# Moving the weight buffers of an fp32r decoder block by 448 bytes: stationary operands 64 bytes behind the moving ones, modulo 512

## The chip, the cores and the metric

The kernel runs on one core of a Trainium2 chip. The metric is the device time of one execution in microseconds (us). Three runs of the kernel before gave 2026.83, 2027.70 and 2027.73 us, a median of 2027.7 us. One more execution was profiled; it has a time of its own, 2027.62 us, and its first to last instruction span 2025.9 us.

## The reference

One layer of a hybrid decoder block over 2048 tokens of 1024 channels, all in float32:

```python
h = rmsnorm(x, norm_g[l])
proj = jnp.einsum("bsd,de->bse", h, w_in[l])          # 1024 -> 7680
glu_in, conv_gate, q, k, v, attn_gate, merge_logits = jnp.split(proj, SPLIT_POINTS, axis=-1)
c = conformer_conv(glu_in, ...)                       # GLU, 31 taps depthwise, layernorm, SiLU
y_conv = jnp.einsum("bsc,cd->bsd", c * jax.nn.silu(conv_gate), w_conv_out[l])
a = sliding_window_attention(q, k, v, attn_sinks[l])  # rope before it; window 128, 16 heads, 4 kv heads
y_attn = jnp.einsum("bsa,ad->bsd", a * jax.nn.silu(attn_gate), w_attn_out[l])
merged = g_conv * y_conv + g_attn * y_attn            # sigmoid gates
x = x + jnp.einsum("bsd,de->bse", merged, w_out[l])
return rmsnorm(x, final_norm_g)
```

## The kernel before, in words

**Tiling.** The tokens are done in two sweeps of 1024 (`T`), each as two halves of 512 (`TH`). The contraction of 1024 channels is cut into 8 chunks of 128 (`KC`). Every product keeps float32 accuracy by splitting both operands into a high part, rounded to fp32r, and a low part, the rest: high times high, high times low and low times high are added up in one PSUM bank. So a projection of 128 output channels over one half is 8 x 3 = 24 matmuls, with a weight load ahead of each; over both halves it is 48 (`project`, lines 267 to 293, the matmul at L281).

**What is stationary, what moves.** In `project` the stationary operand (the weight load) is 128 x 128 numbers of `whi` or `wlo`, and the moving operand is 128 x 512 numbers of `hT` (the normalized input, transposed), `aT` (the gated attention output) or `uT` (the gated convolution output). Per sweep `project` runs for 60 tiles of `w_in`, 8 of `w_attn_out` (named `ya`) and 8 of `w_conv_out` (`yc`): 76 tiles, 152 in the two sweeps. The last product, with `w_out` (L885, named `o`), has it the other way: stationary is `mT`, moving is `wo`, and both lie in slots. So do both operands of the attention products `sc` (L572) and `ov` (L622).

**Memory.** Four pools lie behind each other in each partition: `const`, `slots`, `stage`, `work`. `const` holds `ident_r` (from byte 2,176), `ones` (from 2,688), the parameters and `v_halo` (from 5,952). `slots` is a set of named slots of 4,096 bytes (three of 4,608) which `slot` hands out again and again (lines 81 to 91): `hT`, `aT`, `uT`, `mT`, `wo`, `qk`, `pt`, `vt` and the rest lie there. `stage` has four buffers each of `raw` (a weight tile as it comes from memory), `whi` and `wlo`, 2,048 bytes each. `work` has the half rows `t2k` (five of 2,048 bytes) and small things. In bytes modulo 512 the pools begin like this:

| what | first byte | modulo 512 |
|---|---|---|
| `ident_r`, `ones` (const) | 2,176 and 2,688 | 128 |
| `v_halo` (const) | 5,952 | 320 |
| first slot | 9,024 | 320 |
| last slot, tag `c5` | 182,592 | 320 |
| stage: `raw`, `whi`, `wlo` | 186,688 | 320 |
| work: first `t2k` | 215,424 | 384 |

All slots, all rows of 512 float32 and all columns of 128 float32 are multiples of 512 bytes, so within a pool every operand keeps the number of its pool. The distance that the change is about is that of the stationary operand behind the moving one, modulo 512. In `project` it is 0.

**Order.** TensorE's instructions stand in the order in which the program writes them; a clock of planned time (`Line`, with 0.2275 us per matmul) sets in between them the transposes and the attention's products as they come due, and ScalarE, VectorE and GpSimd get their work at the same points. A weight tile's load from memory, its rounding on ScalarE (L253) and its low part on GpSimd (L242 through `split_lo`) are issued one item ahead of the matmuls that use it (`prefetch` in `project`).

The layernorm's sums over channels are matmuls too (L666): `ones` is stationary and half rows of `work` (`csumh`, `csuml`, `vsumh`, `vsuml`) move.

Of the kernel before, what the change touches and what calls it, by code (L numbers as in the profile page):

```python
# [19 lines left out]
P = 128  # L20
# [33 lines left out]
def hybrid_block(ctx: ExitStack, tc: tile.TileContext, x, par_d, w_in, w_conv, sinks, w_attn, w_out,  # L54
# [22 lines left out]
    C = [f"c{i}" for i in range(8)]  # L77
    X = [f"x{i}" for i in range(3)]
    WIDE = {"c6", "c7", "a14"}

    def slot(tag, shape, dt, name):
        n = int(np.prod(shape[1:]))
        full = 1024 + P if tag in WIDE else 1024
        t = slots.tile([P, full], dt, tag=tag, name=name)
        v = t[:, 0:n]
        if len(shape) == 3:
            v = v.rearrange("p (a b) -> p a b", b=shape[2])
        elif len(shape) == 4:
            v = v.rearrange("p (a b c) -> p a b c", b=shape[2], c=shape[3])
        return v  # L90
# [11 lines left out]
    def load_first(half):  # L102
        xs = []
        for j in range(4):
            r0 = (4 * half + j) * P
            xs.append(slot(A[7 * half + j], [P, D], F32, f"xf{half}_{j}"))
            nc.sync.dma_start(out=xs[-1], in_=x2[r0:r0 + P, :])
        return xs
# [4 lines left out]
    ident_r = const.tile([P, P], F32R, name="ident_r")  # L113
    ident = f(ident_r)
    ident_0 = slot(A[4], [P, P], F32, "ident_0")
    make_identity(nc, ident_0)
    dve.tensor_copy(out=ident_r, in_=ident_0)
    ones_0 = slot(A[5], [P, P], F32, "ones_0")
    dve.memset(ones_0, 1.0 / D)
    ones = const.tile([P, P], F32R, name="ones")  # L120
# [844 lines left out]
```

## Time and profile before

| | |
|---|---|
| median of three runs | 2027.7 us |
| the profiled execution | 2027.62 us, span 2025.9 us |
| TensorE matmul busy (PE) | 2004.9 us, 99% |
| weight loads (PEld) | 1666.9 us, 82% |
| VectorE (DVE) | 1324.1 us, 65% |
| ScalarE (ACT) | 1026.0 us, 51% |
| GpSimd (POOL) | 403.4 us, 20% |
| granted TensorE clock | 0.999 |
| memory traffic | 175 GB/s over the span |

Each row of the group view reads: line, engine, operation, what is written from what (moving operand, then stationary one, for a matmul), shape, count, then busy time in us, the mean ns of one, and the engine's idle time just before them. A matmul's row has a modelled end, so its duration covers the way through the array and overlaps with the next one; the pace of a stream of matmuls is the distance of their starts, and that is read from the timeline, whose first column is the start in us, rounded to 0.01, and whose last is how many instructions of one kind a row holds.

### The profile page before, as it was taken

How to read it: one execution, taken by the hardware profiler on the slowest of the kernel's cores; microseconds unless marked ns; L12 is line 12 of the kernel's file. 1: busy time of each engine (PE TensorE's matmuls, PEld its weight loads, DVE VectorE, ACT ScalarE, POOL GpSimd, SP SyncE). 2: the span in 40 equal slices, each digit the busy share in tenths (PEclk: the TensorE clock that was granted, in tenths of full speed). 3: DMA queues.
4: the chain of work that ended last, by engine and by line, in shares of the span. 5: the costliest groups of instructions: out<-in, count | busy, mean ns of one | idle time of the engine just before them, and what ended most of it. 6: DMA issues, size and time to landing. Idle time of an engine off the chain costs nothing.

```text
span 2025.9 us, 27562 instructions
## 1 busy us (share of the span) xinstructions
PE 2004.9 (99%) x9256; PEld 1666.9 (82%) x9256; DVE 1324.1 (65%) x1965; ACT 1026.0 (51%) x2313; POOL 403.4 (20%) x336
## 2 busy tenths in 40 slices
PE   7999999999999999999999999999999999999998
PEld 6888888888888888888888888888888888888887
DVE  4968779988994365123668678699888924431324
ACT  6312577767777463123533225777777764621222
POOL 2335332333323223241001120110111100001200
PEclk9999999999999999999999999999999999999999
DMA  7445655555566757445343556555555577564432
GB/s 252 146 146 167 212 172 159 161 170 180 161 189 213 245 188 249 150 151 178 134 147 132 167 181 196 159 178 177 176 157 174 175 231 260 176 229 140 152 114 83
DMA packets 265821, 355.91 MB, mean 176 GB/s; under 512 B 28112, under 2 KB 126544, under 8 KB 265680
## 3 DMA queue, kind: packets, MB, share of 16 engines
q1 hardware_dynamic: 265680, 354.16, 53.9%
q8 instruction: 73, 1.20, 0.2%
q14 instruction: 68, 0.56, 0.1%
HBM read 234.51 MB, written 119.54 MB: 175 GB/s over the span
## 4 chain that ended last, share of the span: by engine, by line
PE 94%; DVE 4%; DMA 1%; issue 0%; ACT 0%; SPq 0%; POOL 0%; DVEq 0%; ACTq 0%; POOLq 0%
PE mm_ma L281 9%; PE o L885 9%; PE mm_mc L281 9%; PE mm_yc L281 9%; PE mm_ya L281 9%; PE mm_ga L281 9%; PE mm_gb L281 8%; PE mm_cg L281 8%; PE mm_ag L281 6%; PE mm_q_a L281 4%; PE mm_q_b L281 4%; PE sc L572 3%; DVE acc L396 3%; PE ov L622 2%; PE mm_v L281 2%; PE tpp L602 1%
## 5 line engine op out<-in xcount | busy, mean ns | idle before, releaser
L396 DVE SCALAR_TENSOR_TENSOR acc<-glu,par,acc 128x1024 f32<-128x1024 f32 x464 | 595.9, 1284 | 6.2
L885 PE MATMUL o<-wo,mT 128*128 128x512 f32 x768 | 178.3, 391 | 0.0
L885 PEld LDWEIGHTS o<-wo,mT 128*128 128x128 f32 x768 | 143.1, 188 | 29.2
L281 PE MATMUL mm_cg<-hT,whi_cg 128*128 128x512 f32 x512 | 159.6, 393 | 0.0
L281 PE MATMUL mm_ma<-hT,whi_ma 128*128 128x512 f32 x512 | 159.6, 393 | 0.0
L281 PE MATMUL mm_ga<-hT,whi_ga 128*128 128x512 f32 x512 | 159.4, 392 | 0.2 <-ACT whi_ga L253 0.2
L281 PE MATMUL mm_ag<-hT,whi_ag 128*128 128x512 f32 x512 | 159.4, 392 | 0.0
L281 PE MATMUL mm_gb<-hT,whi_gb 128*128 128x512 f32 x512 | 159.2, 392 | 0.0
L281 PE MATMUL mm_mc<-hT,whi_mc 128*128 128x512 f32 x512 | 157.9, 389 | 0.0
L281 PE MATMUL mm_yc<-uT,whi_yc 128*128 128x512 f32 x512 | 157.7, 389 | 0.0
L281 PE MATMUL mm_ya<-aT,whi_ya 128*128 128x512 f32 x512 | 157.7, 389 | 0.0
L613 POOL TENSOR_SCALAR_AFFINE_SELECT pc<-pt 128x1024 fp32r<-128x1024 f32 x60 | 65.7, 1094 | 422.1 <-DVE pt L242 413.4
L281 PEld LDWEIGHTS mm_ya<-aT,whi_ya 128*128 128x128 f32 x512 | 96.1, 188 | 20.1
L281 PEld LDWEIGHTS mm_yc<-uT,whi_yc 128*128 128x128 f32 x512 | 96.1, 188 | 20.0
L281 PEld LDWEIGHTS mm_mc<-hT,whi_mc 128*128 128x128 f32 x512 | 95.9, 188 | 20.0
L281 PEld LDWEIGHTS mm_ga<-hT,whi_ga 128*128 128x128 f32 x512 | 94.4, 188 | 19.1 <-ACT whi_ga L253 0.6
L281 PEld LDWEIGHTS mm_gb<-hT,whi_gb 128*128 128x128 f32 x512 | 94.6, 188 | 18.6
L281 PEld LDWEIGHTS mm_ag<-hT,whi_ag 128*128 128x128 f32 x512 | 94.2, 188 | 18.3
L281 PEld LDWEIGHTS mm_ma<-hT,whi_ma 128*128 128x128 f32 x512 | 94.1, 188 | 18.1
L281 PEld LDWEIGHTS mm_cg<-hT,whi_cg 128*128 128x128 f32 x512 | 94.0, 188 | 18.1
L592 ACT ACTIVATE ss<-ss,st 128x128 f32<-128x128 f32 x256 | 99.7, 390 | 11.2 <-DVE st L587 10.6
L281 PE MATMUL mm_ga<-hT,wlo_ga 128*128 128x512 f32 x256 | 99.9, 390 | 0.7 <-POOL wlo_ga L242 0.7
(364 smaller groups left out, 4244.5 us busy)
## 6 DMA issues: line engine op xcount, KB each, us to landing
qk<-d_q SPq DMA_DIRECT2D x256, 64.0 KB, 2.2
d_a<-ss SPq DMA_DIRECT2D x128, 128.0 KB, 1.9
aT<-d_a SPq DMA_DIRECT2D x32, 512.0 KB, 5.7
qk<-d_k SPq DMA_DIRECT2D x240, 64.0 KB, 2.0
raw_gb<-in_w_in_dram SPq DMA_DIRECT2D x34, 256.0 KB, 3.4
raw_ga<-in_w_in_dram SPq DMA_DIRECT2D x34, 256.0 KB, 3.3
raw_ag<-in_w_in_dram SPq DMA_DIRECT2D x32, 256.0 KB, 3.6
d_ag<-ag SPq DMA_DIRECT2D x32, 256.0 KB, 2.2
```

Of the source, the lines that this page charges most:

```text
L281: pe.matmul(out=ps, lhsT=a, rhs=b, start=(k == 0 and i == 0), stop=(k == KC - 1 and i == 2))
L396: dve.scalar_tensor_tensor(out=to, in0=glu[c][:, j:j + T], scalar=tap(c, j), in1=acc[c], op0=ALU.mult, op1=ALU.add)
L572: pe.matmul(out=o, lhsT=q[:, h, :], rhs=r, start=(j == 0), stop=(j == 1))
L592: act.activation(out=sb[:, h, :], in_=sb[:, h, :], func=AF.Exp, scale=SCALE, bias=ngm[:, h:h + 1], accum_out=den[:, h:h + 1])
L602: pe.transpose(out=tpp[:, h, :], in_=sb[:, h, :], identity=ident)
L613: pool.affine_select(out=pc, in_=f(pt), pattern=[[0, 2], [0, GQ], [1, P]], compare_op=ALU.is_ge, fill=0.0, base=0, channel_multiplier=-1)
L622: pe.matmul(out=ov, lhsT=vv, rhs=pp[:, i % 2], start=(i == 0), stop=(i == nm - 1))
L885: pe.matmul(out=ps, lhsT=a[:, c0:c0 + P], rhs=r, start=(k == 0 and i == 0), stop=(k == KC - 1 and i == 2))
```

## The change

The slot with the tag `c5` is the last of the pool in memory. It gets 112 float32, that is 448 bytes, more; what is put into it stays as it is.

```diff
     def slot(tag, shape, dt, name):
         n = int(np.prod(shape[1:]))
-        full = 1024 + P if tag in WIDE else 1024
+        full = 1024 + (P if tag in WIDE else 112 if tag == C[5] else 0)
         t = slots.tile([P, full], dt, tag=tag, name=name)
```

All that lies behind that slot moves up by 448 bytes: `stage` begins at 187,136 (256 modulo 512) and the first `t2k` of `work` at 215,872 (320 modulo 512). `const` and all slots stay where they are. No instruction is added, removed or reordered.

## The prediction

> **What bounds the kernel now.** I read the page first: the busy shares, the clock and the chain that ended last.
>
> ```profile
> span 2025.9 us, 27562 instructions
> PE 2004.9 (99%) x9256; PEld 1666.9 (82%) x9256; DVE 1324.1 (65%) x1965; ACT 1026.0 (51%) x2313; POOL 403.4 (20%) x336
> PEclk9999999999999999999999999999999999999999
> PE 94%; DVE 4%; DMA 1%; issue 0%; ACT 0%; SPq 0%; POOL 0%; DVEq 0%; ACTq 0%; POOLq 0%
> ```
>
> TensorE works without a break at its full granted clock, and 94% of the chain that sets the end is its own queue. So the time is the number of matmuls times the pace at which one follows the other, and a change of place in memory matters if it changes that pace. The timeline of TensorE gives the pace in the attention output product, where nothing else is mixed in:
>
> ```profile
> 800.02 0.62 PE L281 MATMUL mm_ya<-aT,whi_ya 128*128 128x512 f32 x2
> 800.47 0.39 PE L281 MATMUL mm_ya<-aT,wlo_ya 128*128 128x512 f32 x1
> ...
> 809.31 0.39 PE L281 MATMUL mm_ya<-aT,wlo_ya 128*128 128x512 f32 x1
> 809.54 0.62 PE L281 MATMUL mm_ya<-aT,whi_ya 128*128 128x512 f32 x2
> ```
>
> Between 800.02 and 809.54 lie 42 matmuls (14 groups of three), 9.52 us, so 226.7 ns each. How much of that is the streaming of 512 columns? Two shapes tell it, in the group view:
>
> ```profile
> L281 PE MATMUL mm_ya<-aT,whi_ya 128*128 128x512 f32 x512 | 157.7, 389 | 0.0
> L572 PE MATMUL sc<-qk 128*128 128x256 f32 x480 | 67.8, 283 | 1.4 <-DVE pt L242 1.3
> L281 PEld LDWEIGHTS mm_ya<-aT,whi_ya 128*128 128x128 f32 x512 | 96.1, 188 | 20.1
> L281 PE MATMUL mm_cg<-hT,whi_cg 128*128 128x512 f32 x512 | 159.6, 393 | 0.0
> ```
>
> 256 columns more take 389 - 283 = 106 ns more, 0.414 ns a column, so 512 columns stream in 212 ns and 226.7 - 212 = 14.7 ns of each step are something else. The attention scores, with half the columns, show the same surcharge:
>
> ```profile
> 500.48 1.11 PE L572 MATMUL sc<-qk 128*128 128x256 f32 x8
> 501.43 0.40 PE L281 MATMUL mm_cg<-hT,whi_cg 128*128 128x512 f32 x1
> ```
>
> Eight of them pass in 0.95 us, 119 ns each, 13 ns over their 106. A weight load takes 188 ns, hidden beside a step of 226.7. So about 15 ns per matmul do not depend on its length; both operands have the same distance (0) in all these groups. Whether those 15 ns are two reads of the memory getting in each other's way, or a fixed price of changing the weights, is what the change asks.
>
> **The change part by part.** It adds no instruction. It changes one distance: of the 76 tiles per sweep of `project`, 48 matmuls each, two sweeps, that is 7,296 matmuls, from 0 to 64 bytes behind. One nanosecond of pace is worth 7.3 us. The 768 matmuls of the output product, the attention products and all tiles in slots keep their distance. I sum up term by term.
>
> *Pace of the 7,296 matmuls.* Nowhere does the trace show a long run at a distance other than 0, but it shows four short ones: the layernorm sums. There `ones` (128 modulo 512) is stationary and a half row of `work` (384) moves, and the last of each four runs while `whi_mc` (320) is loaded for the next, which is 64 bytes behind 384, the very distance of the change.
>
> ```profile
> 697.31 0.39 PE L281 MATMUL mm_mc<-hT,wlo_mc 128*128 128x512 f32 x1
> 697.54 0.39 PE L666 MATMUL lnmu<-csumh,ones 128*128 128x512 f32 x1
> 697.77 0.39 PE L666 MATMUL lnmu<-csuml,ones 128*128 128x512 f32 x1
> 698.00 0.40 PE L666 MATMUL lnmu<-csumh,ones 128*128 128x512 f32 x1
> 698.23 0.39 PE L666 MATMUL lnmu<-csuml,ones 128*128 128x512 f32 x1
> 698.46 0.61 PE L281 MATMUL mm_mc<-hT,whi_mc 128*128 128x512 f32 x2
> 698.91 0.39 PE L281 MATMUL mm_mc<-hT,wlo_mc 128*128 128x512 f32 x1
> ```
>
> The step from 697.31 to 697.54 has `hT` moving and `ones` being loaded, 192 bytes behind: 0.23 us, the usual step as far as 10 ns tell. The four steps from 697.54 to 698.46 take 0.92 us, 230 ns each, 3.3 ns above the usual 226.7; then two steps take 0.45, the usual pace. Nothing here is faster than at distance 0. Read as a price of distance, 3.3 ns x 7,296 = 24 us. But the same slow stretch appears at distance 0, after transposes:
>
> ```profile
> 648.89 0.40 PE L281 MATMUL mm_ma<-hT,wlo_ma 128*128 128x512 f32 x1
> 649.12 0.62 PE L281 MATMUL mm_ma<-hT,whi_ma 128*128 128x512 f32 x2
> 649.58 0.39 PE L281 MATMUL mm_ma<-hT,wlo_ma 128*128 128x512 f32 x1
> 649.81 0.61 PE L281 MATMUL mm_ma<-hT,whi_ma 128*128 128x512 f32 x2
> 650.27 0.39 PE L281 MATMUL mm_ma<-hT,wlo_ma 128*128 128x512 f32 x1
> 650.49 0.61 PE L281 MATMUL mm_ma<-hT,whi_ma 128*128 128x512 f32 x2
> ```
>
> From 648.89 to 649.81 four steps take 0.92 us, just as in the layernorm; from 649.81 to 650.49 three take 0.68, the usual 227. So a disturbance of the stream is paid for by a few slow steps, then the stream falls back into its pace, and the layernorm's four are what such a recovery looks like whatever the distance is. (These spells are why `mm_cg`, mixed with attention, has a mean of 393 ns and `mm_ya` 389.) I take 0 ns for the pace, the value that the nearest steady rows support, with bounds of -14.7 ns (the whole surcharge goes) and +3.3 ns (the stretch at 230 never ends). [...]
>
> *Weights ready in time.* `raw`, `whi`, `wlo` and the half rows shift too, so ScalarE, GpSimd and the DMAs touch other addresses.
>
> ```profile
> L253 ACT CAST whi_yc<-raw_yc 128x512 fp32r<-128x512 f32 x32 | 19.8, 620 | 61.1 <-PE mm_ya L281 34.3 <-issue 22.6 <-DMA wlo_yc<-d_lo 4.2
> L296 ACT CAST uT<-lcg 128x512 fp32r<-128x512 f32 x32 | 19.3, 620 | 28.1 <-DVE lcg L719 27.8
> PE mm_ga L281 <- POOL wlo_ga L242: 0.7, 1, 0.7
> PE mm_ga L281 <- ACT whi_ga L253: 0.2, 1, 0.2
> ```
>
> A cast from 320 to 320 takes 620 ns and one from 384 to 320 takes 620 too, so for ScalarE the place costs nothing, and I take the same for the others. The waits view of TensorE shows 0.9 us in all for weights that were late, in the first tiles of the kernel. Term: 0; if loads became 10 ns slower each, they would still be an item ahead, and cost nothing.
>
> *Transposes and layernorm.* Their stationary or moving tiles in `stage` and `work` shift. The 16 layernorm matmuls cost 3.3 ns each above the pace: 0.05 us, the most that can be won there.
>
> *Sum.* Against the profiled execution: 2027.62 us + 0, its span of 2025.9 with 1.7 us around it. The median of the runs, 2027.7, is the same to 0.1 us. Forecast: 2027.6 us, its own range 2024 to 2032.
>
> **The rivals.** *Collision at equal distance, faster.* The surcharge is a collision of two reads that start at the same number modulo 512, and the weights 64 bytes behind avoid it in part or altogether. For: 14.7 and 13 ns at 512 and 256 columns, at distance 0 in each case; a fixed price that fits one short overlap at the start of each matmul. Against: the step at distance 192 and those at 256 were no faster. If half goes, 7.3 ns x 7,296 = 54 us, 1974 us; if all goes, 14.7 x 7,296 = 107 us, 1920 us. The next engine leaves room for the first: over both attention stages
>
> ```profile
> 240.00:680.00 440.00, 438.59 (x2104) 366.81 (x2103) 360.08 (x552) 315.10 (x771) 135.26 (x113) 1.00 0.57 179
> 1240.00:1700.00 460.00, 460.00 (x2201) 385.05 (x2200) 356.89 (x568) 327.41 (x794) 49.83 (x41) 1.00 0.59 184
> ```
>
> VectorE (the third busy time) is busy 360 of 440 and 357 of 460 us, 82% and 78%; 3% fewer us raise that to 84%. [...]
>
> *A slow pace that stays, slower.* At distance 64 the stream does not fall back: each of the 7,296 steps stays at the 230 ns of the layernorm. Place: all of `project`; price: 3.3 ns, 24 us, 2052 us. It decides as soon as a steady step exceeds 226.7 by 0.6 ns (4 us). For: that is the one place where just this distance stands in the trace, four times, always in a slow stretch. Against: the same stretch at distance 0.
>
> *The change does not do what it says:* the allocator could place the pools otherwise. The pools follow each other without gaps so far, so I give this no more than 0.02, within no change.
>
> **How the numbers follow.** About 0.2% or 4 us is what a measurement of this kernel can tell from no change. No change 0.36; part of the surcharge goes (1974) 0.25; all or nearly all goes (1920 to 1950) 0.11; slow pace (2052) 0.28. As faster, same, slower: 0.36, 0.36, 0.28. The single likeliest case is no change, so 2027.6 us is predicted. The range reaches from 1974 to the slow pace with its reading error: 0.93 in place of 0.92 for four steps is 232.5, 5.8 x 7,296 = 42 us; I take half way, 33 us, 2060. It leaves out the full gain (0.11), and a little on either side.
>
> **What would show it.** In the timeline of the `ya` product three steps take 0.68 us now and if I am right; 0.66 if half of the surcharge goes, 0.64 if all; 0.69 if the slow pace stays. The output product `o` must keep 0.68 in every case, as its distance does not change. If `ya` keeps its pace and the time still moves by more than 4 us, then the shift works through another engine, and the means of the casts (620 ns) and of the DMAs' landing times would show it. If the three steps take 0.66 or less, the step that failed is the one that took the surcharge for a fixed price.

## The result: 1% slower, and the profile after

The kernel with the change takes 2047.92 us (four runs, 2047.66 to 2048.07) against 2027.72 us beside it: 20.2 us more, a ratio of 1.0100 with a 95% interval of 1.0083 to 1.0118. The profiled execution took 2048.03 us, with a span of 2046.3. The time lies within the predicted range, but the forecast, no change, was wrong; the case that happened is the rival with the slow pace (2052 us).

The first lines of the page after, and its chain:

```profile
span 2046.3 us, 27562 instructions
PE 2026.2 (99%) x9256; PEld 1670.1 (82%) x9256; DVE 1326.1 (65%) x1965; ACT 1027.1 (50%) x2313; POOL 404.3 (20%) x336
PE 96%; DVE 2%; DMA 1%; issue 0%; SPq 0%; ACT 0%; POOL 0%; DVEq 0%; POOLq 0%
```

The counts are the same, VectorE, ScalarE and GpSimd are as busy as before to 2 us; only TensorE is busy 21 us longer. The group view says with which matmuls:

```profile
L885 PE MATMUL o<-wo,mT 128*128 128x512 f32 x768 | 178.4, 391 | 0.0
L281 PE MATMUL mm_ya<-aT,whi_ya 128*128 128x512 f32 x512 | 161.5, 397 | 0.0
L281 PEld LDWEIGHTS mm_ya<-aT,whi_ya 128*128 128x128 f32 x512 | 96.8, 189 | 22.7
L253 ACT CAST whi_yc<-raw_yc 128x512 fp32r<-128x512 f32 x32 | 19.8, 620 | 64.8 <-PE mm_ya L281 37.6 <-issue 14.1 <-PE mm_yc L281 10.9
```

A matmul of `ya` has gone from 389 to 397 ns, while `o`, whose operands lie in slots, has its 391 ns as before, the cast its 620 and the weight load 189 for 188. The timeline gives the pace in two places. The first is the middle of the q projections; before the change:

```profile
150.32 0.62 PE L281 MATMUL mm_q_b<-hT,whi_q_b 128*128 128x512 f32 x2
...
157.12 0.62 PE L281 MATMUL mm_q_a<-hT,whi_q_a 128*128 128x512 f32 x2
```

After the change, in the same place and then over the whole `ya` product of the first sweep, which is the second place:

```profile
150.42 0.62 PE L281 MATMUL mm_q_b<-hT,whi_q_b 128*128 128x512 f32 x2
...
157.29 0.62 PE L281 MATMUL mm_q_a<-hT,whi_q_a 128*128 128x512 f32 x2
...
761.04 0.63 PE L281 MATMUL mm_ya<-aT,whi_ya 128*128 128x512 f32 x2
...
850.41 0.40 PE L281 MATMUL mm_ya<-aT,wlo_ya 128*128 128x512 f32 x1
```

From 150.32 to 157.12 lie 30 steps of 226.7 ns, from 150.42 to 157.29 after the change 30 of 229.0. From 761.04 to 850.41 lie 383 steps of 233.3 ns; before, `ya` had 226.7 too. So there are two paces at the same distance. They part at the layernorm, and there at the second of its two sums. The timeline after, from the first sum (`lnmu`) to behind the second (`lnvar`):

```profile
701.08 0.40 PE L666 MATMUL lnmu<-csumh,ones 128*128 128x512 f32 x1
...
703.17 0.39 PE L281 MATMUL mm_mc<-hT,wlo_mc 128*128 128x512 f32 x1
...
738.19 0.39 PE L281 MATMUL mm_mc<-hT,wlo_mc 128*128 128x512 f32 x1
738.42 0.62 PE L281 MATMUL mm_mc<-hT,whi_mc 128*128 128x512 f32 x2
738.88 0.39 PE L281 MATMUL mm_mc<-hT,wlo_mc 128*128 128x512 f32 x1
739.11 0.39 PE L666 MATMUL lnvar<-vsumh,ones 128*128 128x512 f32 x1
...
740.51 0.40 PE L281 MATMUL mm_mc<-hT,wlo_mc 128*128 128x512 f32 x1
740.74 0.63 PE L281 MATMUL mm_mc<-hT,whi_mc 128*128 128x512 f32 x2
741.21 0.40 PE L281 MATMUL mm_mc<-hT,wlo_mc 128*128 128x512 f32 x1
741.44 0.63 PE L281 MATMUL mm_mc<-hT,whi_mc 128*128 128x512 f32 x2
741.91 0.40 PE L281 MATMUL mm_mc<-hT,wlo_mc 128*128 128x512 f32 x1
```

Behind the first sum the stream keeps the milder pace: from 703.17 to 738.19 lie 153 steps of 228.9 ns. Ahead of the second sum three steps take 738.88 - 738.19 = 0.69 us (229 to 230 ns), behind it 741.91 - 741.21 = 0.70 (233). Both sums have their operands at the same places modulo 256, so the distances alone do not say which pace follows. Where the 20.4 us of the span arise is read from the starts of `ya` and `o` in the second sweep, before

```profile
1757.61 0.62 PE L281 MATMUL mm_ya<-aT,whi_ya 128*128 128x512 f32 x2
...
1931.68 0.84 PE L885 MATMUL o<-wo,mT 128*128 128x512 f32 x3
```

and after:

```profile
1772.86 0.63 PE L281 MATMUL mm_ya<-aT,whi_ya 128*128 128x512 f32 x2
...
1952.06 0.85 PE L885 MATMUL o<-wo,mT 128*128 128x512 f32 x3
```

`ya` and `yc` take 179.2 in place of 174.1 us, 5.1 more, which is their 768 steps at 6.7 ns. The first sweep has the same 179.2 (761.04 to 940.24) in place of 174.1 (756.50 to 930.58), so it is in both sweeps 10.2 us. At the start of `o` in the second sweep the kernel is 20.4 us late, and at its end (spans of 2046.3 and 2025.9 us) no more than that. The other 10.2 us lie in the 5,760 remaining matmuls of `project`, 1.8 ns each; that is less than the 2.3 ns from 226.7 to 229.0, as some of them were above 226.7 before already (230 to 233 ns in the rows shown behind transposes and `sc`).

### The profile page after: what moved, and what is told of

The parts are those of the page before. It is cut to its first block, busy times and chain, and to the rows that moved or that the text cites. A ratio compares the mean times of both kernels' runs of the same rounds, so it can differ in the third digit from the quotient of the medians.

```text
span 2046.3 us, 27562 instructions
## 1 busy us (share of the span) xinstructions
PE 2026.2 (99%) x9256; PEld 1670.1 (82%) x9256; DVE 1326.1 (65%) x1965; ACT 1027.1 (50%) x2313; POOL 404.3 (20%) x336
## 4 chain that ended last, share of the span: by engine, by line
PE 96%; DVE 2%; DMA 1%; issue 0%; SPq 0%; ACT 0%; POOL 0%; DVEq 0%; POOLq 0%
PE mm_ya L281 9%; PE mm_yc L281 9%; PE mm_mc L281 9%; PE mm_ma L281 9%; PE mm_cg L281 9%; PE mm_ga L281 9%; PE o L885 9%; PE mm_gb L281 8%; PE mm_ag L281 7%; PE mm_q_a L281 4%; PE mm_q_b L281 4%; PE sc L572 3%; PE ov L622 3%; PE mm_v L281 2%; PE tpp L602 1%; DVE acc L396 1%
## 5 line engine op out<-in xcount | busy, mean ns | idle before, releaser
L281 PE MATMUL mm_ya<-aT,wlo_ya 128*128 128x512 f32 x256 | 101.7, 397 | 0.0
```

Source lines behind the costliest of these rows:

```text
L281: pe.matmul(out=ps, lhsT=a, rhs=b, start=(k == 0 and i == 0), stop=(k == KC - 1 and i == 2))
```

## The experiments

Theory A: the distance of the weight load behind the moving operand sets the pace of TensorE. Rivals: another engine pays (B), the absolute place counts (C), the move itself costs (E), the period is shorter than 512 (F), or the 15 ns over the streaming time are a collision that the right distance avoids (G). Unless it is said otherwise, an experiment changes one number of the kernel before. All of them were timed beside the kernel before, whose medians there were 2027.06 to 2027.69 us; the verdicts on pace come from the `ya` product of the first sweep, last start minus first start over 383 steps.

**Only the stage pool moves** (`e1_stage_only`).

```diff
+    work_pad = work.tile([P, 16], F32, tag="work_pad", name="work_pad", bufs=1)
+    nc.vector.memset(work_pad, 0.0)
-        full = 1024 + P if tag in WIDE else 1024
+        full = 1024 + (P if tag in WIDE else 112 if tag == C[5] else 0)
```

> The last slot is 448 bytes longer as in the change, and 64 more bytes at the head of the work pool bring the half rows of that pool back to their old place modulo 512: only raw, whi and wlo have moved. Theory A, the distance of the weight loads behind the moving operand sets the pace of the matmuls in project: 2046 to 2050 us, and the attention output product keeps its 233 ns per matmul of the changed kernel (226.7 before). Rival B, it is the half rows (layernorm sums, gates, transposes) that cost the time through another engine: 2026 to 2030 us.

2040.13 us, ratio 1.0063 (1.0048 to 1.0078). The weights alone cost 13 us, so A holds against B, but its figures do not: the time is 6 us below its range and 8 us below that of the change, and the pace is not its 233 ns. The timeline of `ya`:

```profile
760.33 0.62 PE L283 MATMUL mm_ya<-aT,whi_ya 128*128 128x512 f32 x2
...
848.00 0.39 PE L283 MATMUL mm_ya<-aT,wlo_ya 128*128 128x512 f32 x1
```

87.67 us for 383 steps, 228.9 ns: at the same distance of the weights the stream has stayed at the milder pace. All that differs from the change is the place of the half rows in `work`, and of the matmuls only the layernorm's and the transposes read those. With the half rows at their old place the layernorm's second sum leaves the stream at 229, with the half rows moved it leaves it at 233.

**Only the work pool moves** (`e2_work_only`).

```diff
+    work_pad = work.tile([P, 112], F32, tag="work_pad", name="work_pad", bufs=1)
+    nc.vector.memset(work_pad, 0.0)
```

> The slots are as before and only the work pool is shifted by 448 bytes; raw, whi and wlo keep distance 0. Theory A: 2026 to 2030 us, pace 226.7 ns in the attention output product. Rival B: 2046 to 2050 us.

2027.53 us, ratio 1.0003 (0.9993 to 1.0013), pace 226.7 ns. At distance 0 the move of the half rows leaves the pace at 226.7 ns: B is out.

**All move together** (`e3_all_together`).

```diff
+    const_pad = const.tile([P, 16], F32, name="const_pad")
+    nc.vector.memset(const_pad, 0.0)
```

> A tile of 64 bytes at the head of the const pool moves everything behind it by 64 bytes; all distances among slots, stage and work stay, the place of each modulo 512 and modulo 128 changes. Theory A, only the distance counts: 2026 to 2030 us, pace 226.7 ns. Rival C, the absolute place counts (the moving rows now begin at a multiple of 128): the pace changes in all groups, the output product among them, to 213 to 220 ns if a crossing of 128 bytes is what costs the 15 ns (1930 to 1975 us).

2027.88 us, ratio 1.0002 (0.9993 to 1.0012), 226.7 ns. A common move of 64 bytes, which also changes the place modulo 128, leaves the pace as it was; C is out for such a move. Smaller common moves were not tried.

**64 bytes ahead in place of behind** (`e4_weights_64_ahead`).

```diff
+        full = 1024 + (P if tag in WIDE else 16 if tag == C[5] else 0)
```

> The last slot is 64 bytes longer in place of 448: the weights lie 64 bytes ahead of the moving tiles. Theory A with a cost that is the same for any distance other than 0: 2040 to 2056 us, as in the change. Theory A with a collision that depends on who is ahead: anything from 1975 to 2040 us, and a pace in the attention output product that is neither 226.7 nor 233 ns. Rival B: 2026 to 2050 us with a pace of 226.7.

2069.89 us, ratio 1.0210 (1.0195 to 1.0225), and 233.3 ns in `ya`. This is worse than either expectation had it: the long stretches of `project` run at the worse pace throughout, and the kernel loses 43 us, 5.9 ns for each of the 7,296 matmuls.

**The period** (`e5_512_longer`, `e6_256_ahead`, `e7_128_ahead`, `e8_128_behind`): the same edit with 128, 64, 32 and 96 in place of 16.

> The last slot is 512 bytes longer: the weights move by as much as in the change and more, but their distance modulo 512 is 0 again. Theory A, the distance modulo 512 sets the pace: 2026 to 2030 us and 226.7 ns per matmul in the attention output product. Rival E, the move itself or the longer slot costs time: 2040 to 2050 us.

> The weights lie 256 bytes from the moving tiles modulo 512. Theory A with a period of 512: a pace other than 226.7 ns, between 225 and 236, 2035 to 2075 us. Rival F, the pattern has a period of 256 or less: 226.7 ns and 2026 to 2030 us.

> The weights lie 128 bytes ahead of the moving tiles. Theory A: a pace other than 226.7 ns; if the price grows with the distance ahead, over 233.3 ns and over 2070 us, and if any distance costs about the same, 229 to 234 ns and 2040 to 2072 us. Rival F with a period of 128: 226.7 ns, 2026 to 2030 us.

> The last slot is 384 bytes longer: the weights lie 128 bytes behind. Theory A: a pace other than that at 64 behind (229.0 or 233.3 ns), 2030 to 2075 us; if weights behind can be ahead of the collision at some distance, this one is the next candidate for a pace below 226.7 ns, under 2020 us. Rival F with a period of 128: 226.7 ns, 2026 to 2030 us.

512 bytes: 2027.28 us, ratio 1.0000 (0.9991 to 1.0009). 256 bytes: 2027.26 us, 1.0000 (0.9990 to 1.0009). 128 ahead: 2064.74 us, 1.0184 (1.0169 to 1.0199). 128 behind: 2064.50 us, 1.0183 (1.0166 to 1.0200). The move and the longer slot cost nothing (E is out). At 256 the kernel is the one before, to 0.3 us, and 128 ahead and 128 behind, which are the same thing modulo 256, give the same time to 0.3 us and the same 232.4 ns. So, as far as these distances show, the period is 256 bytes and not the 512 of the change's description: half of F, as a period of 128 is ruled out. The group view of the run with 256 bytes has the old 389 ns:

```profile
L281 PE MATMUL mm_ya<-aT,whi_ya 128*128 128x512 f32 x512 | 157.7, 389 | 0.0
```

**In between** (`e9_32_ahead`, `e10_32_behind`, `e11_96_ahead`, `e12_96_behind`): the same edit with 8, 56, 24 and 40.

> The weights lie 32 bytes ahead. Theory A', the distance modulo 256 sets the pace, with 0 the best of multiples of 64: if the memory is told apart in steps of 64 bytes, a distance of 32 is half a step, and the pace lies between 226.7 (at 0) and 233.3 ns (at 64): 2035 to 2060 us. Rival G, the 15 ns over the streaming time are a collision that a distance finer than 64 bytes avoids: a pace below 226 ns and under 2020 us. Rival H, only whole 64 bytes count and 32 is the same as 0: 226.7 ns, 2026 to 2030 us.

> The last slot is 224 bytes longer, which is 32 bytes behind modulo 256. Theory A': between 226.7 (at 0) and the 229.0 to 233.3 ns at 64 behind, 2028 to 2050 us. Rival G: below 226 ns, under 2020 us. Rival H: the same as 64 behind or as 0.

> The weights lie 96 bytes ahead. Theory A': between the paces at 64 and 128 ahead, 232 to 234 ns, 2060 to 2075 us. Rival G: below 226 ns, under 2020 us.

> The last slot is 160 bytes longer, which is 96 bytes behind modulo 256. Theory A': between the paces at 64 and at 128 behind, 229 to 233.5 ns, 2038 to 2068 us. Rival G: below 226 ns, under 2020 us.

2069.08, 2068.46, 2076.04 and 2070.75 us, all slower by 2.0 to 2.4%, and each above the range that was expected of theory A'. Theory A's idea of a price that grows in steps of 64 bytes was wrong: 32 ahead cost 41.8 us where 64 ahead cost 42.8, and 32 behind cost 41.1 where the change's 64 behind cost 20.2. That ends rival H as well, by which 32 would be like 0. Rival G found nothing either.

**Finer than 32 bytes** (`e13_16_ahead`, `e14_4_ahead`, `e15_16_behind`): whi and wlo get buffers of 576 float32, so that their distances stay multiples of 256, and begin 4, 1 or 60 float32 into them. The lines for 16 ahead are shown; left out is that `raw_tile`, which uses the same buffers, asks for the longer ones too.

```diff
-            hi = stage.tile([P, 4, P], F32R, tag="whi", name=f"whi_{name}{kh}")
-            lo = stage.tile([P, 4, P], F32R, tag="wlo", name=f"wlo_{name}{kh}")
+            hi = stage.tile([P, TH + 64], F32R, tag="whi", name=f"whi_{name}{kh}")
+            lo = stage.tile([P, TH + 64], F32R, tag="wlo", name=f"wlo_{name}{kh}")
+            hi, lo = (t[:, 4:4 + TH].rearrange("p (a b) -> p a b", b=P) for t in (hi, lo))
```

> The buffers of whi and wlo are 256 bytes longer each, so that their distances stay multiples of 256, and the operand begins 16 bytes into its buffer: weights 16 bytes ahead. Theory A', distance modulo 256 and 0 is the best: a pace of 226.7 to 233.3 ns and 2027 to 2070 us. Rival G, the 15 ns over the streaming time are a collision that a distance finer than 32 bytes avoids: a pace below 226 ns, under 2020 us.

> As the run with 16 bytes, but the operand begins 4 bytes into its buffer: one float32 ahead. If the memory is read in lines of several float32 and a load that straddles them costs more, 2040 us or more; if only whole lines count, 226.7 ns and 2026 to 2030 us. Rival G: under 2020 us.

> The operand begins 240 bytes into a buffer whose length is a multiple of 256: weights 16 bytes behind modulo 256. Theory A': 226.7 to 233.3 ns, 2027 to 2070 us. Rival G: under 2020 us.

16 ahead: 2047.10 us, 1.0095 (1.0080 to 1.0110). 4 ahead: 2063.51 us, 1.0176 (1.0159 to 1.0192). 16 behind: 2033.81 us, 1.0031 (1.0019 to 1.0043). 4 ahead lies in the range of the first of its two cases (2040 us or more); that the memory is read in lines, or that a load straddles them, no run shows. Only the weights move in these runs, so they do not tell whether the distance counts here or the weights' own place within 64 bytes. The run with 16 ahead shows most plainly that the pace depends on more than the distance. Its timeline, in the gate projections beside the attention and in `ya`:

```profile
449.88 0.39 PE L282 MATMUL mm_cg<-hT,wlo_cg 128*128 128x512 f32 x1
...
451.24 0.39 PE L282 MATMUL mm_cg<-hT,wlo_cg 128*128 128x512 f32 x1
...
454.42 0.40 PE L282 MATMUL mm_cg<-hT,wlo_cg 128*128 128x512 f32 x1
...
455.81 0.40 PE L282 MATMUL mm_cg<-hT,wlo_cg 128*128 128x512 f32 x1
...
462.11 0.39 PE L282 MATMUL mm_cg<-hT,wlo_cg 128*128 128x512 f32 x1
462.34 0.60 PE L604 MATMUL tpp<-ident_r,ss 128*128 128x128 f32 x4
...
767.45 0.62 PE L282 MATMUL mm_ya<-aT,whi_ya 128*128 128x512 f32 x2
...
854.26 0.39 PE L282 MATMUL mm_ya<-aT,wlo_ya 128*128 128x512 f32 x1
```

Six steps from 449.88 to 451.24 take 1.36 us, the old pace; then come `ov` and `sc`, and six steps from 454.42 to 455.81 take 1.39, 232 ns. This is no short recovery: the 33 steps from 454.42 to 462.11, up to the next transposes (`tpp`), take 7.69 us, 233.0 ns. And `ya` has 226.7 ns throughout (86.81 us for 383). One distance, two paces, and a disturbance by other matmuls moves the stream from one to the other.

**Only the low part** (`e16_low_part_64_ahead`): the buffers of the last three, whi at their beginning, wlo 16 float32 in.

> Only wlo, one weight load in three, lies 64 bytes ahead; whi keeps distance 0. If each load pays for its own distance: a third of the price of all (42.5 us), 2041 us, with two steps in three at 226.7 ns. If the stream has to find its pace anew after each odd load, as after a transpose, more: up to the full 2070 us, with no step at the old pace.

2053.15 us, ratio 1.0126 (1.0111 to 1.0141): 25.5 us, between 14, a third of the full price, and 43. The timeline of `ya`:

```profile
814.38 0.62 PE L282 MATMUL mm_ya<-aT,whi_ya 128*128 128x512 f32 x2
814.84 0.40 PE L282 MATMUL mm_ya<-aT,wlo_ya 128*128 128x512 f32 x1
815.07 0.62 PE L282 MATMUL mm_ya<-aT,whi_ya 128*128 128x512 f32 x2
...
818.54 0.62 PE L282 MATMUL mm_ya<-aT,whi_ya 128*128 128x512 f32 x2
```

Eighteen steps from 814.38 to 818.54 take 4.16 us, 231.1 ns on average, where one odd step of 233.3 in three would give 228.9. In the same timeline, over the 14 groups of three from 810.22 to 819.92, the step from a start of `wlo` to the next of `whi` takes 235 ns on average, and the two others, from the first `whi` to `wlo`, 229 each. One odd load in three leaves more than one step in three above 226.7: a load does not pay for itself alone.

In one table, by distance modulo 256:

| weights | kernel | `ya` pace, ns | time, us |
|---|---|---|---|
| 0 | before, e2, e3, e5, e6 | 226.7 | 2027.1 to 2027.9 |
| 4 ahead | e14 | 232.4 | 2063.5 |
| 16 ahead | e13 | 226.7 | 2047.1 |
| 32 ahead | e9 | 233.3 | 2069.1 |
| 64 ahead | e4 | 233.3 | 2069.9 |
| 96 ahead | e11 | 234.3 | 2076.0 |
| 128 | e7, e8 | 232.4 | 2064.7, 2064.5 |
| 96 behind | e12 | 233.3 | 2070.8 |
| 64 behind | the change; e1 | 233.3; 228.9 | 2047.9; 2040.1 |
| 32 behind | e10 | 233.3 | 2068.5 |
| 16 behind | e15 | 228.3 | 2033.8 |

No distance is better than 0, and none has a steady pace below 226.7 ns. No kernel was faster than the one before by more than the noise.

The pace of `ya` is not the only one of a kernel at the distances 16 behind and 128 either. At 16 behind (e15), where `ya` has 228.3 ns, the stream between the two layernorm sums has 39 steps in 8.85 us, 226.9 ns:

```profile
702.62 0.39 PE L282 MATMUL mm_mc<-hT,wlo_mc 128*128 128x512 f32 x1
...
711.47 0.39 PE L282 MATMUL mm_mc<-hT,wlo_mc 128*128 128x512 f32 x1
```

At 128 ahead (e7), where `ya` has 232.4 ns, the q projections have 30 steps in 7.00 us, 233.3 ns:

```profile
150.36 0.63 PE L281 MATMUL mm_q_b<-hT,whi_q_b 128*128 128x512 f32 x2
...
157.36 0.63 PE L281 MATMUL mm_q_b<-hT,whi_q_b 128*128 128x512 f32 x2
```

## Why the prediction was wrong, point by point

*What bounds the kernel* was right: TensorE's pace times 7,296 matmuls. So was the worth of a nanosecond, 7.3 us: 20.2 us are 2.8 ns on average.

*The failed step* is the pace term: "I take 0 ns for the pace, the value that the nearest steady rows support". It rested on the reading that the layernorm's four slow steps are what a recovery looks like "whatever the distance is", because the same 0.92 us for four steps appears after transposes at distance 0. The resemblance was real and the conclusion was not. With a period of 256, `ones` at 128 and half rows at 384 are at distance 0: three of the four steps were at distance 0 themselves, and `mm_mc` behind them is at distance 0 as well. So the stretch could not show what a stream does that stays at 64 behind. Its disturbance may have come from the two crossings, `ones` loaded beside `hT` (192 behind, that is 64 ahead) and `whi_mc` loaded beside a half row (64 behind); no run tried them one by one. What the runs showed in place of the 0: at 64 behind the long stretches of `project` never fall back to 226.7 ns; they stay at 229 or 233. At the other distances that are not 0 modulo 256, too, whole stretches stay at 228 to 234 ns.

The transposes were no clean witness for distance 0 either. In those ahead of 648.89 the identity moves (at 128) and `ss` is stationary (in a slot, at 320), which is 64 behind modulo 256. The slow steps behind `sc`, where both operands lie in slots at 320, are the ones that show a recovery at distance 0. In the kernel before:

```profile
501.43 0.63 PE L281 MATMUL mm_cg<-hT,whi_cg 128*128 128x512 f32 x2
501.90 0.39 PE L281 MATMUL mm_cg<-hT,wlo_cg 128*128 128x512 f32 x1
502.13 0.62 PE L281 MATMUL mm_cg<-hT,whi_cg 128*128 128x512 f32 x2
...
647.98 0.60 PE L602 MATMUL tpp<-ident_r,ss 128*128 128x128 f32 x4
```

Three steps from 501.43 to 502.13 take 0.70 us, 233 ns. So a few slow steps after a disturbance do occur at distance 0; that they are all that it costs "whatever the distance is" was the error.

*The bounds.* The +3.3 ns of the stretch were near the truth for the change (2.8 ns on average, made of 1.8 and 6.7), by luck in part: the steady paces are 229.0 and 233.3, not the 230 of the stretch, and the 6.7 ns of `ya` and `yc` lie outside the bound. The -14.7 ns bound was never approached.

*The collision rival*, 0.36 in all, was wrong in its direction: of the places tried the equal one is the best (226.7 ns). The 14.7 ns over the streaming time, an estimate from the row means at 256 and 512 columns (283 and 389 ns), are there at every distance tried, so that surcharge is no collision that a distance in the table avoids; what it is, these runs do not settle. The upper end of the case in which nearly all of it goes, 1950 us, needs a pace of 216 ns. No run shows such a pace: the lowest steady one was 226.7 ns.

*Weights ready in time, ScalarE's indifference, the output product:* right (casts 620 ns, `o` 391 ns, e2 unchanged). *The change does what it says:* right in bytes, but 512 is two periods.

*What the change asked:* with no instruction changed, the distance of the two operands moved the pace of `ya` from 226.7 to as much as 234.3 ns (e11), up to 2.4% of this kernel. Whether the two get in each other's way as reads of the memory, no run shows.

Open: why a stream at distance 64 behind (228.9 and 233.3 ns), 16 ahead (226.7 and 233.0), 16 behind (226.9 and 228.3) or 128 (232.4 and 233.3) has two steady paces, and which of them it takes after a disturbance. That the layernorm's second sum decides it in the change is read from the trace and from e1; why the first sum, with the same operands' places, does not, and what in the chip is behind all this, stays open.

## What to carry to other kernels

In a kernel like this one, with fp32r matmuls of 512 columns and new weights for each, keep the stationary and the moving operand at the same place modulo 256 bytes (226.7 ns a step here); moving the weights to any other distance that was tried cost 0.3 to 2.4%. Read the pace as the distance of starts over a hundred steps or more, in stretches with and without other work between them, since one distance had two paces here (226.7 and 233.0 ns at 16 ahead). And before a short stretch in a trace is used as evidence about a parameter, ask whether the parameter really differs there: the period was not known, and the witness stood at distance 0.

## What the runs showed of the hardware that was not expected

The pace of fp32r matmuls with 512 columns and a weight load each changed with the byte distance of the two operands, with a period of 256 as far as tried: in `ya` 226.7 ns at 0, 256 and 512, 232.4 at 128 on either side, 233.3 to 234.3 at 32, 64 and 96 ahead. At one distance the stream held two paces, 228.9 and 233.3 ns at 64 behind and 226.7 and 233 at 16 ahead, and went from one to the other where other matmuls stand in between (the second layernorm sum at 64 behind; `ov` and `sc` at 16 ahead). A shift by a single float32 (e14) costs 35.8 us, more than a shift by four (19.4 us). The mean of a weight load of `ya`, 187 to 189 ns, barely changes with it.
